# Feed-forward nets of a two-layer decoder: sums moved from GpSimd to VectorE, low parts by adding transfers

## The chip, the cores and the metric

The kernel runs on one core of a Trainium2 chip. The metric is the device time of one execution in microseconds, the median of several runs. TensorE (PE) multiplies, VectorE (DVE), ScalarE (ACT) and GpSimd (POOL) work element by element, SyncE (SP) issues the transfers.

## What is computed

```python
def _swiglu(h, w_gate_up, w_down):
    gu = h @ w_gate_up
    return (jax.nn.silu(gu[..., :D_FF]) * gu[..., D_FF:]) @ w_down
...
    for l in range(DEPTH):
        hn = _rmsnorm(h, attn_norm[l])
        ...
        h = h + _swiglu(_rmsnorm(h, ffn_norm[l]), ffn_w_gate_up[l], ffn_w_down[l])
    return _rmsnorm(h, final_norm)
```

The stream has 1024 tokens of 1024 values in float32, `D_FF` is 2816, and there are two layers: latent attention in layer 0, differential attention in layer 1, each followed by the feed-forward net shown.

## The kernel before

**Numbers in two parts.** TensorE multiplies in `float32r`, which keeps fewer digits than float32. So each operand is held as a high part (the value rounded) and a low part (the value less its high part), and a product takes three matmuls. `split` (L412) makes the two: ScalarE writes the high part, and VectorE, or GpSimd where `sub` says so, subtracts it from the source.

**Fewer products.** The nets use Strassen-Winograd: seven products of half-size blocks in place of eight, with sums of blocks of the weights and of the operands. `block_tail` (L1096) holds one layer's net. Its input is in seven operand lists `x[0]` to `x[6]`. A pair `p` of weight columns goes through `up(p)`: forms 0, 2, 3 and 4 as whole products (accumulators `pa`, `pc`), and form 1, 5 and 6 as `quarter_products`, which apply the scheme once more to 256-column pieces (accumulators `pb`). From pair `CUT` on (pair 4 in layer 0, pair 2 in layer 1) form 1 is in quarters too; before that it is whole. There are eleven pairs per layer. The first three pairs' forms are made ahead, during attention, by `prepare_columns` (L946), and are loaded from memory (`preh`, `prel`).

**Weight forms.** `Columns` makes the forms of a column: it loads blocks into `wr` tiles, `form` (L1237) makes a sum in place (`t` is form 3, then becomes form 2, then form 6), and `get` (L1256) splits it into `wh` and `wl`. With four blocks of rows (`np == 4`, the up weights) the sums ran on GpSimd, else on VectorE. The sums of `quarter_products` (tiles `qt`) ran on GpSimd.

**Down.** After the pairs, `down` and `down_last` multiply the activations by the down weights in four groups. `stage` loads a pair's activations from memory and makes their sums (tiles `stg`), and `place` (L1553) splits the seven of them; forms 2, 4 and 6 had their low parts on GpSimd. VectorE adds every product into the residual tiles `h`.

**Order.** Between `nc.start` and `nc.finish` the calls are only recorded. `Plan.finish` then sets the order on each engine from a table of costs (`Plan.cost`, L287 is the line at which all of them are issued, so L287 stands on almost every row). An engine runs its list in that order: an instruction that waits holds up all behind it on its engine.

Of the kernel before, what the change touches and what calls it, by code (L numbers as in the profile page):

```python
# [14 lines left out]
AF = mybir.ActivationFunctionType  # L15
# [177 lines left out]
class Plan:  # L193
# [100 lines left out]
    def cost(self, engine, name, n, dtype, psum, accum, size):  # L294

        if engine == "tensor":
            if name == "transpose":
                return 0.107, self.HOP
            return n * (1 if dtype == F32R else 6 if n <= 64 else 8) / 2400, self.HOP
        if engine == "scalar":  # L300
            return (0.05 if psum else 0.09) + n / 1200 + 0.19 * accum, self.HOP
        if engine == "vector":
            return 0.067 + n / 960 + 0.063 * (name == "scalar_tensor_tensor" and not psum), self.HOP
        if engine == "gpsimd":
            return (0.245 + n / 1200 if name == "tensor_scalar" else 0.15 + n / 475), self.HOP
        return max(0.45, size / 360e3), 2.2
# [64 lines left out]
def trunk(ctx: ExitStack, tc: tile.TileContext, A: dict):  # L371
# [34 lines left out]
    def f32(ap):  # L406
        return ap.bitcast(F32)
# [4 lines left out]
    def split(dst_hi, dst_lo, src, scale=1.0, sub=None):  # L412
        nc.scalar.activation(dst_hi, src, AF.Copy, scale=scale)
        if isinstance(scale, float) and scale == 1.0:
            (sub or nc.vector).tensor_tensor(dst_lo, src, f32(dst_hi), ALU.subtract)
        else:
            nc.vector.scalar_tensor_tensor(dst_lo, src, scale, f32(dst_hi), ALU.mult, ALU.subtract)

    def mm3(ps, parts):
        n = len(parts)  # L420
# [532 lines left out]
    def prepare_columns(layer, j, tags):  # L953


        kept = pre[layer, j] = {i: [dram.tile([P, HF], F32R, name="pre" + part) for part in "hl"] for i in early_forms(layer, j // 2)}
        t4 = kept["t4"] = dram.tile([P, HF], F32, name="pret")

        def load(i):
            t = tags.tile([P, HF], F32, "pb", "pb")  # L960
            nc.sync.dma_start(out=t, in_=A["wgu"][layer, j, :, i])
            return t

        def keep(i, src):
            pair = [tags.tile([P, HF], F32R, "p" + part, "p" + part) for part in "hl"]
            split(*pair, src, sub=nc.gpsimd)
            for d, t in zip(kept[i], pair):
                move(d, t)

        def sub(dst, a, b):  # L970
            nc.gpsimd.tensor_tensor(dst, a, b, ALU.subtract)

        t = tags.tile([P, HF], F32, "pt", "pt")
        nc.sync.dma_start(out=t, in_=A["wgu"][layer, j, :, 1])
        b0 = load(0)
        sub(t, t, b0)
        keep(0, b0)
        yield
        keep(3, t)
        b3 = load(3)  # L980
        sub(t, b3, t)
        yield
        keep(2, t)
        b2 = load(2)
        sub(t, b2, t)
        nc.sync.dma_start(out=t4, in_=t)
        yield
        if 1 in kept:
            keep(1, b2)
            yield  # L990
        b1, b3 = load(1), load(3)
        sub(b1, b3, b1)
        keep(4, b1)
        yield
# [135 lines left out]
    def block_tail(layer, half, resid, last, side_work=None, ahead=None, meanwhile=None):  # L1130
# [90 lines left out]
        class Columns:  # L1221
# [16 lines left out]
            def form(self, j):  # L1238
                if self.made is not None and j == 6:
                    return raw(self.made["t4"])  # L1240
                eng = nc.gpsimd if self.np == 4 else nc.vector
                b = self.block
                if j == 3:
                    self.t = raw()
                    return self.sub(self.t, b(1), b(0), eng)
                if j == 2:
                    return self.sub(self.t, b(3), self.t, eng)
                if j == 4:
                    return self.sub(b(1), b(3), b(1), eng)
                if j == 6:  # L1250
                    return self.sub(self.t, b(2), self.t, eng)
                return b({0: 0, 1: 2, 5: 3}[j])

            def get(self, i):
                if self.made is not None and self.forms[i] is None:
                    self.forms[i] = wtile()  # L1256
                    for t, d in zip(self.forms[i], self.made[i]):
                        move(t, d)
                while self.forms[i] is None:
                    j = next(self.order)  # L1260
                    src = self.form(j)
                    w = self.np * P
                    hi, lo = (t[:, :w] for t in (self.kept[j]() if j in self.kept else wtile()))
                    split(hi, lo, src[:, :w])
                    self.forms[j] = hi, lo
                return self.forms[i]

# [30 lines left out]
        def quarter_products(i, w0, w1, d0, d1):  # L1298

            t13, t24 = htile(7, 1, "qt"), htile(6, 1, "qt")  # L1300
            nc.gpsimd.tensor_tensor(t13[:, L], w1[:, L], w0[:, L], ALU.subtract)
            nc.gpsimd.tensor_tensor(t13[:, R], w1[:, R], w1[:, L], ALU.subtract)
            nc.gpsimd.tensor_tensor(t24[:, L], w1[:, R], t13[:, L], ALU.subtract)
            nc.gpsimd.tensor_tensor(t24[:, R], w0[:, R], t24[:, L], ALU.subtract)
            ws = []
            for s in (w0, t13, t24, w1):
                w = wtile()
                c = R if s is w1 else slice(0, HF)
                split(*(t[:, c] for t in w), s[:, c])
                ws.append(w)  # L1310
            part = lambda w, c: [t[:, c] for t in w]
            b11, b21, b22 = part(ws[0], L), part(ws[0], R), part(ws[3], R)
            t1, t3, t2, t4 = part(ws[1], L), part(ws[1], R), part(ws[2], L), part(ws[2], R)
            a11, a12, s4, a22, s1, s2, s3 = quarters[i]

            def mul(ps, xs, w, start):
                for k, (xh, xl) in enumerate(xs):
                    wh, wl = (t[:, k * P : (k + 1) * P] for t in w)
                    nc.tensor.matmul(ps, lhsT=wh, rhs=xh, start=start and k == 0, stop=False, skip_group_check=not start)
                    nc.tensor.matmul(ps, lhsT=wh, rhs=xl, start=False, stop=False, skip_group_check=not start)  # L1320
                    nc.tensor.matmul(ps, lhsT=wl, rhs=xh, start=False, stop=k == 1, skip_group_check=not start)

            def add(t, ps):
                nc.vector.tensor_tensor(t, t, ps, ALU.add)

            c11, c12, c21, c22 = d0[:, L], d1[:, L], d0[:, R], d1[:, R]
            a, b, c = (bank("pb")[:, L] for _ in range(3))
            mul(a, a11, b11, True)
            add(c11, a)
            mul(b, a12, b21, True)  # L1330
            add(c11, b)
            mul(c, s1, t1, True)
            add(c22, c)
            mul(a, s2, t2, False)
            add(c12, a)
            mul(c, s4, b22, False)
            add(c12, c)
            mul(a, s3, t3, False)
            add(c22, a)
            mul(a, a22, t4, False)  # L1340
            add(c21, a)
# [211 lines left out]

        def place(xs, p, i):
            t = dtile(i, SLOTS[p])
            split(*t, staged[p][i], sub=nc.vector if i in (0, 1, 3, 5) else nc.gpsimd)
            xs[i].append(t)


# [4 lines left out]
        for k in range(4):  # L1564
            a21, a22 = h[1][k], h[1][k + 4]
            for t, kk in ((a21, k), (a22, k + 4)):
                nc.vector.scalar_tensor_tensor(t, t, gain(f"ffn{layer}", kk), r, ALU.mult, ALU.mult)
            s1, s2 = (tags.tile([P, HF], F32, "st", "st") for _ in range(2))
            a11, a12 = h[0][k], h[0][k + 4]
            forms = [a11, a12, s2, s1, a21, a12, a22]  # L1570
            for _ in sums(a11, a12, a21, a22, s1, s2, a12, (nc.vector, nc.gpsimd)):
                pass
            for i in range(2, 5):
                x[i][k] = xtile(i, k)
                split(*x[i][k], forms[i], sub=nc.vector if i < 4 else nc.gpsimd)
        for _ in range(6):
            next(ups[0])
        for _ in range(4):
# [1 line left out]
        for i, src in ((5, h[0][4:]), (6, h[1][4:])):  # L1580
            for k in range(4):
                x[i][k] = xtile(i, k)
                c = L if k < 2 else slice(0, HF)
                split(*(t[:, c] for t in x[i][k]), src[k][:, c], sub=nc.vector if i == 5 else nc.gpsimd)
            quarter_operands(i, src.__getitem__, nc.vector if i == 5 else nc.gpsimd)

        def whole(k):

# [395 lines left out]
```

## Time and profile before

| | us |
|---|---|
| runs | 2487.7, 2488.48, 2494.13; median 2488.48 |
| the profiled execution, its own time | 2489.24 |
| its span in the trace | 2487.0 |
| TensorE busy | 2334.4 (94%) |
| VectorE busy | 1928.1 (78%) |
| ScalarE busy | 1167.5 (47%) |
| GpSimd busy | 1124.2 (45%) |

Busy times overlap, so they don't add up to the span. TensorE is busy for nearly all of it; the question of every stage is what TensorE waits for in the rest. The nets lie at 503 to 1180 us (layer 0) and 1790 to 2452 us (layer 1) of the span: in each the pairs come first and the down product last.

### The profile page before, as it was taken

The numbers are of one execution on the slowest core, as the hardware profiler recorded it, in microseconds if no ns is written. First come the engines' busy times: TensorE is split into PE (matmuls) and PEld (weight loads), VectorE is DVE, ScalarE is ACT, GpSimd is POOL, SyncE is SP. The second block draws the span as 40 slices with busy tenths as digits, with TensorE's granted clock in tenths as the row PEclk, the third lists the DMA queues.
The fourth block names the chain that finished last, engine by engine and source line by source line (L and its number), as shares of the span: only waits on it lengthen the run. The fifth ranks groups of instructions, "written<-read, shape, count | busy, mean of one in ns | idle before, by whom it ended". The sixth has DMA issues, their size and how long they took to land. (4 is left out here: it accounts for less than half of the span.)

```text
span 2487.0 us, 38148 instructions
## 1 busy us (share of the span) xinstructions
PE 2334.4 (94%) x12776; PEld 1998.5 (80%) x12776; DVE 1928.1 (78%) x3685; ACT 1167.5 (47%) x2323; POOL 1124.2 (45%) x979
## 2 busy tenths in 40 slices
PE   9989999989899997999999999999889999988997
PEld 7879898768788886777889898888678888876776
DVE  7855564597978789999686767676688787799997
ACT  5356554344444444343465555454344444454442
POOL 3256532262656552123377765443365565542212
PEclk9999999999999999999999999999999999999999
DMA  6166673746322235322376653463834222244321
GB/s 185 43 204 200 200 247 110 229 134 209 97 79 91 75 106 185 104 92 88 95 220 196 212 167 118 142 224 109 278 115 147 79 88 77 82 151 152 103 67 70
DMA packets 202003, 346.36 MB, mean 139 GB/s; under 512 B 24656, under 2 KB 57680, under 8 KB 201808
## 3 DMA queue, kind: packets, MB, share of 16 engines
q1 hardware_dynamic: 201808, 343.93, 44.0%
q8 instruction: 101, 1.65, 0.3%
q14 instruction: 94, 0.77, 0.1%
HBM read 239.89 MB, written 95.03 MB: 135 GB/s over the span
## 5 line engine op out<-in xcount | busy, mean ns | idle before, releaser
L287 ACT ACTIVATE wh<-wr 128x512 fp32r<-128x512 f32 (+2 forms) x530 | 287.3, 550 | 443.6 <-PE pb L287 130.8
L287 DVE TENSOR_TENSOR wl<-wr,wh 128x512 fp32r<-128x512 f32 (+2 forms) x530 | 393.1, 755 | 32.8 <-ACT wh L287 32.2
L287 PE MATMUL pa<-xh,wh 128*128 128x512 f32 (+1 forms) x850 | 339.0, 400 | 34.7 <-DVE h L287 14.7
L287 PE MATMUL pa<-xh,wl 128*128 128x512 f32 (+1 forms) x850 | 337.3, 398 | 17.7 <-DVE wl L287 16.4
L287 PE MATMUL pa<-xl,wh 128*128 128x512 f32 (+1 forms) x850 | 336.0, 396 | 4.3 <-DVE xl L287 4.3
L287 PE MATMUL pb<-xh,wh 128*128 128x256 f32 (+1 forms) x976 | 291.9, 302 | 23.0 <-DVE s L287 17.1
L287 PE MATMUL pb<-xl,wh 128*128 128x256 f32 (+1 forms) x976 | 291.1, 299 | 0.0
L287 PE MATMUL pb<-xh,wl 128*128 128x256 f32 (+1 forms) x976 | 290.0, 299 | 0.1
L287 POOL TENSOR_TENSOR wr<-wr 128x512 f32<-128x512 f32 x128 | 179.0, 1398 | 173.5 <-DMA wr<-wgu 85.2
L287 POOL TENSOR_TENSOR xl<-stg,xh 128x512 fp32r<-128x512 f32 x66 | 110.3, 1688 | 305.2 <-ACT xh L287 164.7
L287 PEld LDWEIGHTS pa<-xh,wh 128*128 128x128 f32 x850 | 162.9, 192 | 76.7 <-DVE h L287 15.1
L287 PEld LDWEIGHTS pb<-xh,wh 128*128 128x128 f32 x976 | 186.3, 192 | 45.7 <-DVE s L287 26.4
L287 PEld LDWEIGHTS pa<-xh,wl 128*128 128x128 f32 x850 | 162.4, 191 | 56.3 <-DVE wl L287 24.0
L287 PEld LDWEIGHTS pb<-xl,wh 128*128 128x128 f32 x976 | 187.1, 192 | 13.5
L287 PEld LDWEIGHTS pb<-xh,wl 128*128 128x128 f32 x976 | 186.3, 192 | 6.2 <-DVE wl L287 0.8
L287 PEld LDWEIGHTS pa<-xl,wh 128*128 128x128 f32 x850 | 163.0, 192 | 35.0 <-DVE xl L287 6.0
L287 POOL TENSOR_SCALAR p<-p,tot 128x640 f32<-128x640 f32 (+7 forms) x128 | 99.0, 774 | 182.5 <-DVE tot L287 119.2
L287 ACT ACTIVATE p<-sc,nmax 128x128 f32<-128x128 f32 (+7 forms) x192 | 141.9, 741 | 78.0 <-DVE nmax L287 46.1
L287 POOL TENSOR_TENSOR qt<-wr 128x256 f32<-128x256 f32 x120 | 102.9, 877 | 125.6 <-DVE wl L287 108.0
L287 PE MATMUL pc<-xh,wh 128*128 128x512 f32 x352 | 138.8, 397 | 9.0 <-DVE h L287 8.8
L287 DVE TENSOR_TENSOR s<-s,pb 128x256 f32<-128x256 f32 (+1 forms) x278 | 115.4, 425 | 38.5 <-PE pb L287 35.4
L287 PE MATMUL pc<-xl,wh 128*128 128x512 f32 x352 | 139.6, 397 | 3.0 <-DVE xl L287 3.0
(296 smaller groups left out, 6496.9 us busy)
## 6 DMA issues: line engine op xcount, KB each, us to landing
wr<-wgu SPq DMA_DIRECT2D x142, 256.0 KB, 3.2
act_d<-s SPq DMA_DIRECT2D x88, 256.0 KB, 2.7
stg<-act_d SPq DMA_DIRECT2D x88, 256.0 KB, 3.0
wr<-wd SPq DMA_DIRECT2D x96, 192.0 KB, 2.4
pb<-wgu SPq DMA_DIRECT2D x60, 256.0 KB, 3.9
preh<-ph SPq DMA_DIRECT2D x58, 256.0 KB, 3.1
prel<-pl SPq DMA_DIRECT2D x58, 256.0 KB, 2.7
wh<-preh SPq DMA_DIRECT2D x58, 256.0 KB, 4.8
```

What stands on the lines that cost most here:

```text
L287: return getattr(getattr(self.nc, engine), name)(*map(put, args), **{k: put(a) for k, a in kw.items()})
```

## The change

```diff
@@ Plan.cost
+        if name == "dma_start" and engine == "gpsimd":
+            return 0.9, 3.8
@@ new, beside split
+    def low_by_transfer(dst_hi, dst_lo, src):
+
+        nc.scalar.activation(dst_hi, src, AF.Copy)
+        nc.scalar.activation(dst_lo, src, AF.Copy, scale=-1.0)
+        nc.gpsimd.dma_start(out=f32(dst_lo), in_=src, accum_op=ALU.add)
@@ prepare_columns
-            nc.gpsimd.tensor_tensor(dst, a, b, ALU.subtract)
+            nc.vector.tensor_tensor(dst, a, b, ALU.subtract)
@@ Columns.form, Columns.get
-                eng = nc.gpsimd if self.np == 4 else nc.vector
+                eng = nc.vector
-                    split(hi, lo, src[:, :w])
+                    (low_by_transfer if self.np == 4 else split)(hi, lo, src[:, :w])
@@ quarter_products (four lines like this one)
-            nc.gpsimd.tensor_tensor(t13[:, L], w1[:, L], w0[:, L], ALU.subtract)
+            nc.vector.tensor_tensor(t13[:, L], w1[:, L], w0[:, L], ALU.subtract)
@@ place
-            split(*t, staged[p][i], sub=nc.vector if i in (0, 1, 3, 5) else nc.gpsimd)
+            if i in (2, 6):
+                low_by_transfer(*t, staged[p][i])
+            else:
+                split(*t, staged[p][i], sub=nc.vector)
@@ operands before the first pair
-            for _ in sums(a11, a12, a21, a22, s1, s2, a12, (nc.vector, nc.gpsimd)):
+            for _ in sums(a11, a12, a21, a22, s1, s2, a12, (nc.vector, nc.vector)):
-                split(*x[i][k], forms[i], sub=nc.vector if i < 4 else nc.gpsimd)
+                (split if i < 4 else low_by_transfer)(*x[i][k], forms[i])
-                split(*(t[:, c] for t in x[i][k]), src[k][:, c], sub=nc.vector if i == 5 else nc.gpsimd)
-            quarter_operands(i, src.__getitem__, nc.vector if i == 5 else nc.gpsimd)
+                split(*(t[:, c] for t in x[i][k]), src[k][:, c])
+            quarter_operands(i, src.__getitem__, nc.vector)
```

With `low_by_transfer` ScalarE writes the rounded value and then the rounded value negated, and a transfer issued from GpSimd adds the source to the second: the low part is the same as before.

In the whole program the instructions of TensorE are the same in number. GpSimd loses 530 tensor instructions and gains 182 transfers: 130 of whole weight forms (`wl<-wr`), 44 of staged activations (`xl<-stg`), 8 of operands (`xl<-h`). ScalarE gains 182 activations of 128x512. VectorE loses 130 low parts of 128x512 (`wl<-wr,wh`) and gains 218 sums or low parts of 128x512, 48 of them in attention, and 260 of 128x256, 240 of them the `qt` sums.

The plan makes a new order out of it. GpSimd, end of the list, the last pairs and the down product of layer 1; before:

```order
L287 TENSOR_TENSOR wr<-wr 128x512 x4
L287 TENSOR_TENSOR xl<-stg,xh 128x512
L287 TENSOR_TENSOR qt<-wr 128x256 x2
L287 TENSOR_TENSOR qt<-wr,qt 128x256
L287 TENSOR_TENSOR xl<-stg,xh 128x512
L287 TENSOR_TENSOR qt<-wr,qt 128x256
L287 TENSOR_TENSOR xl<-stg,xh 128x512 x31
L287 TENSOR_TENSOR ss<-ss,sq 128x512 x6
```

and in the change, from the operands of layer 1's net to the same place:

```order
L287 TENSOR_TENSOR xl<-h,xh 128x512 x8
L287 DMA xl<-h 128x512 x4
L287 TENSOR_TENSOR whole<-xh,xl 128x512 x4
L287 DMA wl<-wr 128x512 x64
L287 DMA xl<-stg 128x512 x22
L287 TENSOR_TENSOR ss<-ss,sq 128x512 x6
```

Between the operands and the last norm GpSimd now holds the four `whole` sums of form 1 and transfers, nothing else.

VectorE in the change, a stretch between two pairs of layer 1, with what each waits for (DMASW is a semaphore of a transfer issued from GpSimd; `s_22265` collects a pair's gate):

```order
L287 TENSOR_TENSOR wr<-wr 128x512 [waits DMASW2_49]
L287 TENSOR_TENSOR s_22265<-s_22265,pb 128x256 [waits PE_49]
L287 TENSOR_TENSOR s_22265<-s_22265,pb 128x256 [waits DVE_49,PE_49]
L287 TENSOR_TENSOR s_22265<-s_22265,pb 128x256 [waits PE_49]
L287 TENSOR_TENSOR wr<-wr 128x512 [waits DMASW4_49]
L287 TENSOR_TENSOR wl<-wr,wh 128x512 [waits Activation_49]
L287 TENSOR_TENSOR wl<-qt,wh 128x512 [waits Activation_49]
```

The sums in place now stand in VectorE's list among the additions that set TensorE's accumulators free, and they wait for the transfer that still reads the tile.

ScalarE in the change at the start of a pair (`pa_22152` is the accumulator of the pair before, `wl_22534` the low part of the new pair's form 0):

```order
L287 ACTIVATE s2_22484<-pa_22152 128x512
L287 ACTIVATE wh_22518<-wr_22311 128x512
L287 ACTIVATE sg_22527<-pa_22152 128x512
L287 ACTIVATE wl_22534<-wr_22311 128x512
L287 ACTIVATE wh_22542<-wr_22354 128x512
L287 ACTIVATE wl_22552<-wr_22354 128x512
```

Ahead of the second half of such a pair's low part stands the copy `sg` of the last whole product. In TensorE's list 48 quarter matmuls (128x256) and 4 whole ones (128x512) lie between the last matmul of that product and the first that reads `wl_22534`.

## Rows read from the trace of the kernel before

**Rows 1.** The page, its span and TensorE's busy time.

```profile
span 2487.0 us, 38148 instructions
...
PE 2334.4 (94%) x12776; PEld 1998.5 (80%) x12776; DVE 1928.1 (78%) x3685; ACT 1167.5 (47%) x2323; POOL 1124.2 (45%) x979
```

**Rows 2.** Stages: length, busy PE, PEld, DVE, ACT, POOL; clock, DMA share, GB/s.

```profile
503.00:594.00 91.00, 79.95 (x406) 66.27 (x405) 78.15 (x132) 40.13 (x79) 49.07 (x46) 0.96 0.49 158
594.00:679.00 85.00, 77.41 (x415) 66.50 (x414) 76.54 (x131) 36.11 (x68) 44.54 (x43) 0.98 0.39 119
679.00:905.00 226.00, 221.45 (x1301) 193.35 (x1300) 177.55 (x289) 107.32 (x187) 124.66 (x117) 1.00 0.28 84
905.00:960.00 55.00, 43.34 (x239) 36.90 (x238) 50.36 (x81) 29.50 (x58) 28.08 (x21) 0.94 0.52 170
960.00:1180.00 220.00, 203.48 (x858) 161.81 (x857) 210.09 (x353) 87.53 (x171) 54.77 (x37) 0.98 0.33 105
1250.00:1660.00 410.00, 392.29 (x2435) 349.50 (x2434) 300.01 (x753) 226.94 (x504) 246.17 (x216) 0.98 0.57 177
...
1790.00:1880.00 90.00, 78.07 (x406) 65.43 (x406) 78.40 (x121) 39.43 (x79) 53.63 (x50) 0.96 0.49 156
1880.00:2186.00 306.00, 300.68 (x1768) 262.63 (x1767) 244.37 (x400) 145.75 (x259) 167.10 (x157) 1.00 0.30 91
2186.00:2242.00 56.00, 45.05 (x242) 38.54 (x241) 50.47 (x82) 29.94 (x59) 28.78 (x21) 0.92 0.51 167
2242.00:2452.00 210.00, 196.14 (x832) 156.72 (x831) 200.64 (x343) 83.32 (x164) 46.63 (x30) 0.98 0.30 91
```

**Rows 3.** TensorE's waits over the span: us in total, times, longest.

```profile
PE pb L287 <- DVE s L287: 17.1, 7, 6.2
PE pa L287 <- DVE wl L287: 16.4, 17, 3.2
```

**Rows 4.** Timeline between two pairs of layer 1: start, duration, engine, what.

```profile
1960.06 0.32 SPq L287 DMA_DIRECT2D act_d<-s  x1
...
1960.72 1.28 POOL L287 TENSOR_TENSOR wr<-wr 128x512 f32<-128x512 f32 x1 [1.23 <-DVE wl L287]
1960.89 1.65 DVE L287 TENSOR_TENSOR wl<-wr,wh 128x512 fp32r<-128x512 f32 x1
...
1961.24 0.28 PE L287 MATMUL pb<-xl,wh 128*128 128x256 f32 x1
...
1961.36 0.28 PE L287 MATMUL pb<-xh,wl 128*128 128x256 f32 x1
...
1962.60 0.50 PE L287 MATMUL pa<-xh,wl 128*128 128x512 f32 x1 [0.60 <-DVE wl L287]
```

**Rows 5.** Groups by form, whole span: count, busy us, mean ns, idle before.

```profile
L287 DVE TENSOR_TENSOR wl<-wr,wh 128x512 fp32r<-128x512 f32 x258 | 232.2, 909 | 32.4 <-ACT wh L287 31.9 <-issue 0.2
...
L287 ACT ACTIVATE wh<-wr 128x512 fp32r<-128x512 f32 x258 | 162.3, 630 | 213.8 <-PE pb L287 95.7 <-DMA wr<-wo 33.4 <-POOL wr L287 32.0
...
L287 DVE TENSOR_TENSOR s<-s,pb 128x256 f32<-128x256 f32 x266 | 107.5, 413 | 36.9 <-PE pb L287 35.1
...
L287 DVE TENSOR_TENSOR wl<-qt,wh 128x512 fp32r<-128x512 f32 x120 | 102.6, 867 | 25.5 <-ACT wh L287 25.4
...
L287 DVE TENSOR_TENSOR h<-h,pa 128x512 f32<-128x512 f32 x136 | 90.5, 677 | 12.5 <-PE pa L287 12.2
...
L287 DVE TENSOR_TENSOR s<-s,sg 128x512 f32<-128x512 f32 x44 | 53.5, 1242 | 1.3 <-ACT sg L287 1.3
```

**Rows 6.** The same view, VectorE in the down product of layer 0 (960 to 1180 us).

```profile
L287 DVE TENSOR_TENSOR wl<-wr,wh 128x384 fp32r<-128x384 f32 x78 | 47.6, 623 | 0.1
...
L287 DVE TENSOR_TENSOR xl<-stg,xh 128x512 fp32r<-128x512 f32 x32 | 29.4, 932 | 0.0
```

**Rows 7.** Transfers: issue, count, KB each, median us from issue to landing.

```profile
wr<-pret SPq DMA_DIRECT2D x12, 256.0 KB, 5.5
...
out<-h SPq DMA_DIRECT2D x8, 256.0 KB, 2.0
```

More of the change, by code (lines that the diff above doesn't have):

```diff
@@ L1300, in quarter_products @@
             t13, t24 = htile(7, 1, "qt"), htile(6, 1, "qt")
-            nc.gpsimd.tensor_tensor(t13[:, L], w1[:, L], w0[:, L], ALU.subtract)
-            nc.gpsimd.tensor_tensor(t13[:, R], w1[:, R], w1[:, L], ALU.subtract)
-            nc.gpsimd.tensor_tensor(t24[:, L], w1[:, R], t13[:, L], ALU.subtract)
-            nc.gpsimd.tensor_tensor(t24[:, R], w0[:, R], t24[:, L], ALU.subtract)
+            nc.vector.tensor_tensor(t13[:, L], w1[:, L], w0[:, L], ALU.subtract)
+            nc.vector.tensor_tensor(t13[:, R], w1[:, R], w1[:, L], ALU.subtract)
+            nc.vector.tensor_tensor(t24[:, L], w1[:, R], t13[:, L], ALU.subtract)
+            nc.vector.tensor_tensor(t24[:, R], w0[:, R], t24[:, L], ALU.subtract)
             ws = []
```

## The prediction

> **What bounds the kernel now.** I read the page first, then busy times by stage, then TensorE's waits, a timeline at one of them, and the groups by form. TensorE is busy for 94% of 2487.0 us [rows 1], so no change of the other engines can give back more than its idle time and what a lowered clock costs. The stages say where that lies [rows 2]: length less TensorE's busy time is 11.1, 7.6, 4.6, 11.7 and 16.5 us in the five stages of layer 0's net, and 11.9, 5.3, 11.0 and 13.9 us in the four of layer 1's, 93.4 us together. A clock column below 1.00 means that part of the stage ran at 1.2 GHz instead of 2.4; a share of 0.96 over 91 us is a loss of 0.04 x 91 = 3.6 us. Over the same nine stages this is 3.6 + 1.7 + 0 + 3.3 + 4.4 + 3.6 + 0 + 4.5 + 4.2 = 25.3 us. So 119 us is the ceiling in the nets; the low clock stands in the stages with idle time and not in the two without long waits.
>
> What TensorE waits for there is VectorE: additions that empty accumulators, and low parts [rows 3]. In the down products it is busy 210.1 of 220 us and 200.6 of 210 us, 96%, which makes it the bound of those stages; between pairs in the middle of the nets it has 177.6 of 226 us and room [rows 2].
>
> And VectorE is slowed by GpSimd. At 1960.72 us GpSimd starts a subtraction; the low part that VectorE starts at 1960.89 takes 1.65 us, and TensorE waits 0.60 us for it [rows 4]. With one operand in PSUM the same size takes 677 ns on average; the three forms with both operands in SBUF take 909, 867 and 1242 ns [rows 5]. Excess over 677: 258 x 0.232 + 120 x 0.190 + 44 x 0.565 = 59.9 + 22.8 + 24.9 = 107.6 us. The Trainium skill has this as a rule (SBUF — State Buffer, section Who interferes with whom): a VectorE instruction with two SBUF inputs and a GpSimd instruction that reads SBUF exclude each other for a whole instruction. The trace agrees, with 1.65 us against 0.677.
>
> **The change part by part.** *VectorE's sum.* In the nets, besides what attention gets, 218 - 48 - 130 = 40 instructions of 128x512 more, at 0.677, and 260 of 128x256 at 0.413 [rows 5]: 27.1 + 107.4 = 134.5 us. Against it stand the 107.6 us of excess and that of smaller groups, two of which I read in one down product [rows 6]: 32 x (0.932 - 0.677) = 8.2 us, and 78 x (0.623 - 0.545) = 6.1 us, where 0.545 is halfway between 0.413 and 0.677. VectorE therefore gets no less work in the whole. What changes is where and when: the 240 `qt` sums lie in the pairs, where VectorE has room, and the excess leaves the down products and the turns, where it has none.
>
> *Down products.* Per layer nine `place` calls of form 4 come to VectorE there, 9 x 0.677 = 6.1 us; 14.3 us of excess go by the two rows named, more by the others. VectorE's net relief is 8 us of 220 by these two rows, more by groups not read. While it is 96% busy TensorE's waits on it shrink by about as much, and with them the low clock. Lost there are 16.5 + 4.4 and 13.9 + 4.2 us; I take 10 us per layer: **-20** (bounds 0 and -39).
>
> *Turns from pairs to down* (905 to 960, 2186 to 2242 us). Lost: 11.7 + 3.3 and 11.0 + 4.5 us, most of it in single waits of up to 6.2 us on `s` [rows 3] behind VectorE's list. Three low parts in seven leave GpSimd, one of them for VectorE. I take a third: **-10** (bounds 0 and -30).
>
> *First pairs* (503 to 679, 1790 to 1880 us). VectorE has 78 of 91 us and gets about 8 sums of 0.677 and 28 of 0.413, 17 us per layer; the excess that leaves here I did not count. Of 14.7 + 9.3 + 15.5 us lost I take **-5** (bounds +10 and -20).
>
> *Steady pairs.* Lost are 4.6 + 5.3 us [rows 2], in waits like the one of 0.60 us shown [rows 4]. Now the low part of form 0 comes through ScalarE and a transfer. TensorE has 48 quarter and 4 whole matmuls to do meanwhile; quarters follow each other by 0.12 us [rows 4], whole ones by twice that: 6.7 us. Of these ScalarE takes two activations, 2 x 0.63 = 1.3 us less a little overlap [rows 5], so about 5.5 us remain for issue and landing. The trace has no transfer from GpSimd and none that adds. Bounds for 256 KB: 2.0 us, the quickest, and 5.5 us, the slowest [rows 7]; for the issue 0.32 us, SP's, and 1.28 us, a whole GpSimd instruction [rows 4]. I take 4.0, twice the quick one because two tiles are read, and 0.9: 4.9 us, in time. So less than half of what is lost comes back: **-4** (bounds -10 and, at 5.5 + 1.28, +1.3 us in each of the 16 pairs whose forms are not made ahead = +21).
>
> The Trainium skill prices a GpSimd transfer alone at 2.0 us plus bytes over 436 GB/s (DMA: Bandwidth & Descriptors, section Anatomy of one DMA — SWDGE path), an estimate of 2.6 us here; by it the transfer would be in time as well, and no run yet shows it.
>
> *ScalarE.* 182 activations of 0.63 us are 115 us; it is idle for half of each stage (145.8 busy of 306) [rows 2], so they are hidden but come ahead of copies of accumulators: **+2** (bounds 0 and +15). *DMA.* Its share is 0.28 to 0.30 in the steady pairs [rows 2]; eight more transfers per pair hide in that, and loads of `wr` wait for them: **+3** (bounds 0 and +12).
>
> *Attention.* 48 sums go from GpSimd to VectorE, 33 us at 0.677, up to 79 us if each is stopped as in [rows 4], because softmax work stays on GpSimd. In layer 1 VectorE is busy 300 of 410 us [rows 2], so there is cover; without it they would cost their length. **+3** (bounds -5 and +15).
>
> Sum: -20 - 10 - 5 - 4 + 2 + 3 + 3 = -31 us on 2489.24 us, the profiled execution's own time (2.2 us over its span, 0.8 us over the median): **2458 us**.
>
> **The rivals.** *Late transfers (slower).* If issue and landing take 7.5 us, form 0 is late by 2.0 us in 16 pairs, and the next form, which has about 1 us more time, by about 1.0: 48 us. VectorE suffers too: its sums in place wait for the same transfers, and the additions to `s` that TensorE needs stand behind them. With the gain of 31 kept elsewhere at 27: 2489 + 48 - 27 = 2510 us. It decides from about 6.4 us on, where 0.9 x 16 plus a little on the second form and VectorE's waits eats the 27. For it: rows of 5.5 us exist; against: quiet DMA queues in these stages.
>
> *Only moved (no change).* VectorE's 134.5 us of new work is as much as the excess that leaves; if the new list meets the accumulators as badly, the waits merely stand elsewhere: 2485 to 2493 us. For it: the sum above; against: the down products, where the balance is clearly downward.
>
> *GpSimd still blocks.* If issuing a transfer stops VectorE as a subtraction did, 182 issues of 0.9 us are 164 us, and with half of that as excess VectorE's list grows by 82 + 134.5 - 107.6 = 109 us. In the steady pairs it has 48 and 62 us of room [rows 2], in the other stages almost none; if a quarter reaches TensorE, that is 27 us: 2516 us. For it: both are work of GpSimd; against: an issue is short (SP's 0.32 us) beside a subtraction's 1.28 [rows 4]. The Trainium skill has a trap of the reverse kind (SBUF — State Buffer, The "DVE blocks DMA" trap): VectorE in two-port modes starves GpSimd of writing descriptors, and `tensor_tensor` has no such mode; if it held here, the transfers would be late, the first rival.
>
> **How the numbers follow.** The forecast has 64 in 100, with its own range of 2415 to 2480; late transfers 16, only moved 13, GpSimd still blocks 5, and 2 for attention or the first pairs costing more than the rest gives (2500 us). Within 0.3% of 2488 us (7.5 us), about what a measurement of this kernel can tell from no change, lies "only moved": 0.13. Faster by more is the forecast, 0.64; slower are the other three, 0.23. The range takes in the ceiling's two thirds, 2489 - 79 = 2410, and the first rival's 2510.
>
> **What would show it.** In the changed profile the groups of two SBUF operands should fall to about 680 ns, VectorE's busy share in the down products to about 90%, its idle time there should show, and TensorE's idle time in down and turns should fall by about a third or half. TensorE's waits should not name `wl<-wr` transfers. The prediction is wrong if landings of the adding transfers come later than 5 us, if VectorE's waits name them, or if the 909 ns stay.

## The result, and the profile after

The change takes 2426.56 us, median of four runs (2422.76 to 2435.62), against 2491.11 us before in the runs beside them: a ratio of 0.975, 95% interval 0.9726 to 0.9774. It is faster by 2.5%, twice the forecast's size and inside its range. The profiled execution took 2435.62 us, the slowest of its four, so the two traces differ by 53 us and the medians by 64.6. The sizes below are those of the traces.

The page of the change, as [rows 1], and its DMA queues (packets, MB, share of 16 engines' span):

```profile
span 2433.7 us, 38359 instructions
...
PE 2316.3 (95%) x12776; PEld 1994.8 (82%) x12776; DVE 1876.3 (77%) x4033; ACT 1246.4 (51%) x2505; POOL 663.6 (27%) x631
...
q1 hardware_dynamic: 201808, 343.93, 44.4%
q0 software_dynamic: 26208, 47.72, 11.5%
```

To compare stages I cut both traces at the same points of the work, the issues of the same `act_d<-s` transfers. Before, cut in this way (columns as in [rows 2]): six steady pairs of layer 0, its turn to the down product and that product, then eight pairs of layer 1, its turn and its down product.

```profile
679.00:911.00 232.00, 226.97 (x1335) 197.98 (x1333) 183.55 (x297) 111.67 (x195) 129.02 (x120) 1.00 0.28 86
911.00:961.00 50.00, 38.83 (x207) 33.02 (x208) 45.36 (x74) 25.15 (x50) 24.73 (x17) 0.92 0.52 170
961.00:1179.00 218.00, 201.48 (x850) 160.15 (x849) 208.71 (x349) 86.90 (x170) 53.53 (x36) 0.98 0.34 106
1883.00:2192.00 309.00, 303.62 (x1786) 264.93 (x1784) 247.37 (x401) 147.52 (x261) 171.12 (x159) 1.00 0.29 91
2192.00:2242.00 50.00, 39.11 (x204) 33.54 (x205) 44.47 (x74) 25.54 (x51) 24.02 (x17) 0.91 0.52 171
2242.00:2456.00 214.00, 200.14 (x866) 160.72 (x865) 202.88 (x348) 85.20 (x168) 47.87 (x32) 0.98 0.30 90
```

The change, the same six stages:

```profile
669.00:893.00 224.00, 222.96 (x1335) 198.47 (x1335) 171.00 (x369) 128.88 (x241) 41.27 (x48) 1.00 0.61 142
893.00:937.00 44.00, 39.37 (x217) 33.09 (x215) 37.14 (x77) 30.99 (x62) 8.58 (x10) 0.96 0.87 237
937.00:1150.00 213.00, 202.71 (x854) 162.09 (x854) 200.17 (x366) 94.82 (x188) 30.55 (x28) 0.97 0.48 136
1859.00:2153.00 294.00, 293.38 (x1757) 261.53 (x1756) 225.53 (x488) 170.25 (x317) 52.26 (x60) 1.00 0.60 142
2153.00:2194.00 41.00, 38.18 (x217) 32.02 (x215) 37.14 (x78) 30.66 (x62) 8.71 (x10) 1.00 0.90 246
2194.00:2403.00 209.00, 198.45 (x871) 160.55 (x872) 194.65 (x364) 92.94 (x186) 23.23 (x24) 0.98 0.44 122
```

The pairs in the middle are shorter by 8 and 15 us, the turns by 6 and 9, the down products by 5 each. Read layer 0's pairs: 1335 matmuls are recorded in both, and TensorE's *busy* time fell with its idle time, by 4.0 and 4.0 us. VectorE gives layer 0's down product 200 us of 213, 94%; whether it is still the bound there is what e9 tests.

TensorE's waits in the change (as [rows 3]):

```profile
PE pb L287 <- DVE wl L287: 12.7, 2, 6.3
...
PE pa L287 <- DVE h L287: 11.5, 6, 4.2
...
PE pa L287 <- DVE wl L287: 4.6, 8, 1.3
...
PE pa L287 <- DMA wl<-wr: 2.9, 3, 1.9
...
PE pb L287 <- DVE s L287: 2.0, 3, 1.0
```

The 17.1 us on `s` are 2.0 now, the 16.4 on `wl` 4.6. The first two rows hold new waits: two of 6.3 us, one in the first pairs of each layer, and one of 4.2 us, below. VectorE's groups by form (as [rows 5]), over the span:

```profile
L287 DVE TENSOR_TENSOR wl<-wr,wh 128x512 fp32r<-128x512 f32 x128 | 98.1, 773 | 60.0 <-ACT wh L287 58.4 <-PE psp L287 0.5 <-issue 0.4
L287 DVE TENSOR_TENSOR wr<-wr 128x512 f32<-128x512 f32 x128 | 87.8, 687 | 20.1 <-DMA wl<-wr 11.9 <-DMA wr<-wgu 8.1
L287 DVE TENSOR_TENSOR wl<-qt,wh 128x512 fp32r<-128x512 f32 x120 | 82.7, 691 | 0.4 <-ACT wh L287 0.4
```

and in layer 0's down product, 937 to 1150 us (as [rows 6]):

```profile
L287 DVE TENSOR_TENSOR wl<-wr,wh 128x384 fp32r<-128x384 f32 x78 | 44.5, 586 | 0.0
L287 DVE TENSOR_TENSOR h<-h,pa 128x512 f32<-128x512 f32 x66 | 44.2, 681 | 11.5 <-PE pa L287 7.8 <-DMA h<-h_mid 3.4
L287 DVE TENSOR_TENSOR xl<-stg,xh 128x512 fp32r<-128x512 f32 x45 | 30.5, 702 | 0.0
```

The 867 and 932 ns are 691 and 702; the 773 ns over the span mix in attention, where GpSimd still works. The adding transfers (as [rows 7]):

```profile
wl<-wr POOLq DMA_DIRECT2D x130, 256.0 KB, 4.5
...
xl<-stg POOLq DMA_DIRECT2D x44, 256.0 KB, 4.5
```

The timeline at three places of layer 1 (as [rows 4]): an issue on GpSimd, four matmuls of a pair, the start of the down product.

```profile
1967.80 0.76 DVE L287 TENSOR_TENSOR qt<-wr 128x256 f32<-128x256 f32 x2
...
1968.23 0.89 POOL L287 DMA_DIRECT2D wl<-wr  x1 [0.66 <-PE pa L287]
1968.47 0.42 DVE L287 TENSOR_TENSOR qt<-wr,qt 128x256 f32<-128x256 f32 x1
...
1978.48 0.39 PE L287 MATMUL pa<-xh,wl 128*128 128x512 f32 x1
1978.71 0.39 PE L287 MATMUL pa<-xh,wh 128*128 128x512 f32 x1
1978.94 0.39 PE L287 MATMUL pa<-xl,wh 128*128 128x512 f32 x1
1979.16 0.39 PE L287 MATMUL pa<-xh,wl 128*128 128x512 f32 x1
...
2196.86 0.69 DVE L287 TENSOR_TENSOR h<-h,pa 128x512 f32<-128x512 f32 x1 [4.45 <-DMA h<-h_mid]
...
2197.60 0.80 PE L287 MATMUL pa<-xh,wh 128*128 128x512 f32 x1 [4.17 <-DVE h L287]
```

The issue lies beside two sums, and neither is longer for it. The matmuls are 0.39 us long in the trace and follow each other by 0.23: one that starts up to 0.16 us late leaves no idle time at all. Adding up by how much each start comes after the regular distance (0.227 us behind a 128x512 matmul, 0.114 to 0.117 behind a 128x256) shows the size of it: in the steady pairs before, TensorE started 9.1 and 10.8 us late in all, of which only 4.5 and 5.2 us show as idle; in the change it is 1.8 and 1.3 us.

### The profile page after: what moved, and what is told of

Same layout as the page of the kernel before. It is cut to its first block, busy times and chain, and to the rows that moved or that the text cites. A ratio compares the mean times of both kernels' runs of the same rounds, so it can differ in the third digit from the quotient of the medians.

```text
span 2433.7 us, 38359 instructions
## 1 busy us (share of the span) xinstructions
PE 2316.3 (95%) x12776; PEld 1994.8 (82%) x12776; DVE 1876.3 (77%) x4033; ACT 1246.4 (51%) x2505; POOL 663.6 (27%) x631
## 3 DMA queue, kind: packets, MB, share of 16 engines
q1 hardware_dynamic: 201808, 343.93, 44.4%
q0 software_dynamic: 26208, 47.72, 11.5%
## 4 chain that ended last, share of the span: by engine, by line
PE 73%; DVE 13%; DMA 8%; issue 2%; ACT 2%; POOL 1%; SPq 1%; DVEq 0%; POOLq 0%; ACTq 0%
PE pa L287 22%; PE pb L287 14%; PE pc L287 8%; PE psp L287 7%; PE sc L287 5%; PE psv L287 4%; PE pswo L287 4%; PE pso L287 4%; DVE h L287 2%; PE tp L287 2%; DVE wl L287 2%; PE acc L287 1%; DVE xl L287 1%; PE psr L287 1%; PE ps L287 1%
## 5 line engine op out<-in xcount | busy, mean ns | idle before, releaser
L287 PE MATMUL pa<-xh,wh 128*128 128x512 f32 (+1 forms) x850 | 333.7, 397 | 18.3 <-DVE h L287 11.3
L287 PE MATMUL pa<-xh,wl 128*128 128x512 f32 (+1 forms) x850 | 330.7, 395 | 8.3 <-DVE wl L287 4.6
L287 DVE TENSOR_TENSOR wl<-wr,wh 128x384 fp32r<-128x384 f32 (+2 forms) x400 | 233.8, 596 | 81.9 <-ACT wh L287 80.3
L287 POOL DMA_DIRECT2D wl<-wr x130 | 112.6, 889 | 483.1 <-ACT wl L287 270.2
L287 PEld LDWEIGHTS pb<-xh,wl 128*128 128x128 f32 x976 | 185.6, 191 | 19.6 <-DVE wl L287 13.5
L287 DVE TENSOR_TENSOR wr<-wr 128x512 f32<-128x512 f32 (+2 forms) x256 | 154.1, 607 | 20.2 <-DMA wl<-wr 11.9
L287 PE MATMUL pc<-xh,wl 128*128 128x512 f32 x352 | 139.0, 395 | 3.0 <-DVE wl L287 2.7
```

The costliest lines, as they stand in the source:

```text
L287: return getattr(getattr(self.nc, engine), name)(*map(put, args), **{k: put(a) for k, a in kw.items()})
```

## The experiments

Two theories. *Reads*: the gain is that GpSimd no longer reads SBUF beside VectorE's sums. *Transfers*: it is that whole low parts have left VectorE. The table has all kernels; stage lengths are read at the same cuts as above, in us, layer 0 plus layer 1 (first pairs: four and three; steady pairs: six and seven; the attention between the nets), and can be off by 1 us. All but the before row have the ratio to the runs of before on the same chip.

| kernel | median, us | ratio, 95% interval | first pairs | steady pairs | turns | downs | attention |
|---|---|---|---|---|---|---|---|
| before | 2488 to 2491 | | 184+136 | 232+271 | 50+50 | 218+214 | 606 |
| the change | 2426.56 | 0.975, 0.9726 to 0.9774 | 172+137 | 224+258 | 44+41 | 213+209 | 608 |
| e1_sums_only | 2448.1 | 0.9841, 0.9825 to 0.9857 | 171+136 | 223+257 | 41+41 | 221+216 | 613 |
| e2_transfers_only | 2540.14 | 1.0211, 1.0194 to 1.0227 | 187+134 | 260+314 | 47+47 | 210+206 | 610 |
| e3_reads_beside | 2499.94 | 1.0052, 1.0033 to 1.007 | 216+165 | 221+257 | 42+42 | 213+208 | 604 |
| e4_writes_beside | 2429.13 | 0.9761, 0.9746 to 0.9775 | 169+135 | 222+257 | 43+42 | 212+209 | 607 |
| e5_attention_back | 2438.58 | 0.98, 0.978 to 0.982 | 172+137 | 223+258 | 43+43 | 210+207 | 619 |
| e6_down_weights_too | 2483.15 | 0.9978, 0.9961 to 0.9994 | 173+135 | 223+258 | 42+40 | 237+233 | 604 |
| e7_first_operands_back | 2428.76 | 0.9762, 0.9741 to 0.9784 | 175+136 | 221+258 | 43+42 | 211+210 | 607 |
| e8_staged_back | 2457.07 | 0.9877, 0.9856 to 0.9898 | 172+138 | 222+258 | 48+47 | 221+217 | 606 |
| e9_staged_all_by_transfer | 2434.89 | 0.9788, 0.9773 to 0.9803 | 171+136 | 224+258 | 42+41 | 213+212 | 607 |
| e10_plan_counts_later | 2452.16 | 0.9851, 0.9834 to 0.9867 | 173+133 | 235+268 | 50+48 | 208+206 | 606 |
| e11_plan_counts_earlier | 2433.19 | 0.977, 0.9753 to 0.9787 | 175+135 | 225+261 | 42+43 | 212+207 | 605 |
| e12_quarter_sums_back | 2448.76 | 0.9843, 0.9825 to 0.9861 | 177+136 | 221+268 | 48+47 | 211+208 | 606 |

**The two halves apart.** e1: every adding transfer is a `split` on VectorE again.

```diff
-                    (low_by_transfer if self.np == 4 else split)(hi, lo, src[:, :w])
+                    split(hi, lo, src[:, :w])
```

> All the change's sums on VectorE, but every low part by a VectorE subtraction, no transfer. It leaves GpSimd as free of reading SBUF in the nets as the change does, and VectorE gets 182 more subtractions of 0.68 us, 124 us. Theory A (the gain is that VectorE is no longer stopped by GpSimd): groups with two SBUF operands at about 0.69 us as in the change, and most of the gain in the steady pairs where VectorE had 23% of its time free; with 8 x 0.68 = 5.4 us more work in a pair of 37 us VectorE stays just under its limit: 2435 to 2465 us. Theory B (the gain is the work that the transfers take from VectorE): no gain or a loss, 2490 us or more.

It keeps 40 of the 62 us that the ratio of the change stands for. VectorE's groups are as quick as in the change, though its list is longer:

```profile
L287 DVE TENSOR_TENSOR xl<-stg,xh 128x512 fp32r<-128x512 f32 x154 | 102.4, 688 | 0.0
L287 DVE TENSOR_TENSOR h<-h,pa 128x512 f32<-128x512 f32 x136 | 90.3, 677 | 8.4 <-PE pa L287 7.9
```

Pairs and turns are as short as in the change; the downs are 437 us, longer than before (432). So taking the sums and low parts off GpSimd makes the gain in pairs and turns by itself, and the transfers make that in the downs. The attention is 5 us longer than in the change, and why is open. e2: the sums are on GpSimd again, the transfers stay.

```diff
-                eng = nc.vector
+                eng = nc.gpsimd if self.np == 4 else nc.vector
```

> All low parts that the change gives to transfers, but the sums stay on GpSimd as before. VectorE loses 130 subtractions, 88 us. Theory A: groups with two SBUF operands stay slow (over 0.8 us) and the time is 2465 to 2490 us. Theory B: most of the gain is here, 2425 to 2445 us.

Slower than before, which no theory said. The groups stay slow as A had it (`wl<-qt` 883 ns); the downs are short, the steady pairs 71 us longer than before. GpSimd's groups by form show what is new:

```profile
L287 POOL TENSOR_TENSOR wr<-wr 128x512 f32<-128x512 f32 x128 | 173.7, 1358 | 204.0 <-DMA wl<-wr 183.4 <-issue 7.8 <-DMA wr<-wgu 6.5
```

A sum in place waits on GpSimd for the transfer that still reads its tile, 183.4 us in all, and the next issues stand behind it. The delay can be followed to TensorE: in layer 1's steady pairs GpSimd waits 82.6 us for `wl<-wr`, ScalarE 46.5 us for GpSimd's `wr`, and TensorE 19.1 us for ScalarE's `wh`.

**Reads and writes of GpSimd.** e3 adds two sums on a 128x256 scratch tile, which nothing reads, behind every adding transfer in the code; e4 three fills of the tile.

```diff
         nc.gpsimd.dma_start(out=f32(dst_lo), in_=src, accum_op=ALU.add)
+        for _ in range(2):
+            nc.gpsimd.tensor_tensor(idle[0], idle[0], idle[0], ALU.add)
```

> The change, with two additions of a 128x256 scratch tile on GpSimd (0.74 us each before) after each of the 182 transfers; they read and write SBUF and feed nothing. Theory A: the two-operand groups of VectorE rise from 0.69 us to 0.78 or more, TensorE waits for low parts and sums again, and 182 x 1.5 us of GpSimd work take back a third or more of the gain: 2445 to 2475 us. Theory B: GpSimd has over 70% idle in the nets, the time stays within 0.4% of 2427 us.

> The same, with three fills of the scratch tile on GpSimd in place of the two additions: GpSimd is as busy or nearly so, writes SBUF and reads nothing. If what stops VectorE is GpSimd's reading, two-operand groups stay at 0.69 us and the time at 2427 us within 0.4%. If any work on GpSimd stops it (or delays the issue of the transfers), it loses as much as the run with additions.

The scratch work has no input but itself, so the plan set much of it early: 168 of e3's 364 sums, and 153 of e4's 546 fills, in layer 0's first pairs. So they do not lie beside each transfer, and the test is what happens where they do lie. e3, its groups from 500 to 715 us:

```profile
L287 POOL TENSOR_TENSOR idle<-idle 128x256 f32<-128x256 f32 x168 | 131.0, 780 | 11.6
...
L287 DVE TENSOR_TENSOR wl<-qt,wh 128x512 fp32r<-128x512 f32 x18 | 16.3, 913 | 0.3 <-ACT wh L287 0.2
L287 DVE TENSOR_TENSOR xl<-h,xh 128x256 fp32r<-128x256 f32 x20 | 15.5, 811 | 0.0
```

The change, from 500 to 669 us:

```profile
L287 DVE TENSOR_TENSOR xl<-h,xh 128x256 fp32r<-128x256 f32 x20 | 7.5, 417 | 0.4 <-ACT xh L287 0.4
```

e4, in the same stretch:

```profile
L287 POOL MEMSET idle<- 128x256 f32 x153 | 54.5, 356 | 7.4
...
L287 DVE TENSOR_TENSOR wl<-qt,wh 128x512 fp32r<-128x512 f32 x18 | 12.1, 683 | 2.8 <-ACT wh L287 2.8
L287 DVE TENSOR_TENSOR xl<-h,xh 128x256 fp32r<-128x256 f32 x20 | 7.5, 416 | 0.0
```

Beside reads the 128x256 low part takes 811 ns, beside fills 416, and 417 in the change. All of e3's loss lies in the first pairs, 44 and 28 us longer than in the change; no other stage is longer by more than 1 us. It is VectorE that TensorE waits for there, 29.7 us in layer 0's, and transfers `wl<-wr` only 3.1 us, so a late issue is not what costs. With fills nothing is lost. The fills kept GpSimd busy for 54.5 of 169 us and the sums for 131.0 of 215, so they are about half as dense, but nothing of the slowing is left. The Trainium skill (SBUF — State Buffer, section Who interferes with whom) says this: a VectorE instruction with two SBUF inputs contends with a GpSimd instruction that reads SBUF, not with one that only writes it. Both runs agree, with 811 and 416 ns. Only 10 of e3's sums lie in the steady pairs and none in the turns and downs, so it speaks for the first pairs alone.

**Parts undone one by one.** e5: the sums of the forms made ahead, in attention.

```diff
 prepare_columns
-            nc.vector.tensor_tensor(dst, a, b, ALU.subtract)
+            nc.gpsimd.tensor_tensor(dst, a, b, ALU.subtract)
```

> The change, with the 48 sums of the weight forms made ahead, which lie in attention, back on GpSimd; all else as in the change. A, the prediction's term: these sums cost VectorE 33 us of length that attention covers, and their move was worth between -5 and +5 us: 2421 to 2432 us, the groups of the nets unchanged at about 690 ns. B, rival: attention is where GpSimd's reads hurt as well, since VectorE has two-operand work there too; then the time rises by 10 us or more, 2437 or above, and the mean of VectorE's two-operand groups in attention rises above 800 ns.

12 us slower, by the time theory B; the attention between the nets takes 619 us in place of 608. But B's cause is not shown: `wl<-wr` there has 869 ns in both kernels, and TensorE's waits name one of 7.0 us at the start of layer 1's attention that neither the change nor before has:

```profile
PE sc L287 <- DVE ks L369: 7.0, 1, 7.0
```

Before, with these sums on GpSimd, attention took 606 us. What the part is worth depends on the order around it; its cause stays open. e7: the first operands (half of the sums, low parts of forms 4 to 6, quarter operands of form 6).

```diff
-            quarter_operands(i, src.__getitem__, nc.vector)
+            quarter_operands(i, src.__getitem__, nc.vector if i == 5 else nc.gpsimd)
```

> The change, with the operands ahead of the first pair (half of the sums, the low parts of forms 4 to 6, the quarter operands of form 6) back on GpSimd. A: the two waits of 6.3 us for a first quarter's low part come from VectorE's longer list there and go away; the first pairs of layer 1 get their 4 us back: 2415 to 2424 us. B, rival: GpSimd's reads come back beside VectorE's work in the first pairs and cost as much as the list did: 2425 to 2445 us, with VectorE's groups between the net's start and the third pair again at 900 ns or more.

The same time as the change, in the range of B. The two waits of 6.3 us go, as A said, and two on `s` come (9.2 us in all, 4.7 the longest). GpSimd's reads do slow VectorE again, as B said: the eight low parts `xl<-st` of layer 0 take 1430 ns in place of 685. So the part is worth nothing either way. e8: the staged low parts.

```diff
-            if i in (2, 6):
-                low_by_transfer(*t, staged[p][i])
-            else:
-                split(*t, staged[p][i], sub=nc.vector)
+            split(*t, staged[p][i], sub=nc.vector if i in (0, 1, 3, 5) else nc.gpsimd)
```

> The change, with the low parts of staged activations 2, 4 and 6 back on GpSimd as before. A: the down products' and turns' gain, some 25 us for the two layers, comes from these low parts leaving GpSimd: 2440 to 2455 us, low parts in the down products at 900 ns and more, the down products at about 218 and 214 us. B, rival: VectorE's list is the bound of the down products in either case, so what stopping costs it is given back by the shorter list: 2420 to 2432 us; then the gain of the down products has another source.

A, and a little more than its range: 31 us slower by the medians; in the trace turns are 9 and downs 17 us longer.

```profile
L287 DVE TENSOR_TENSOR xl<-stg,xh 128x512 fp32r<-128x512 f32 x88 | 74.8, 860 | 0.0
```

VectorE is busy for 212.4 us of layer 0's down product with 357 instructions, where the change has 200.2 with 366. e12: the `qt` sums.

```diff
-            nc.vector.tensor_tensor(t13[:, L], w1[:, L], w0[:, L], ALU.subtract)
+            nc.gpsimd.tensor_tensor(t13[:, L], w1[:, L], w0[:, L], ALU.subtract)
```

> The change, with the 240 sums qt of the quarter products back on GpSimd; the sums of the weight forms stay on VectorE. A: GpSimd's reads in the pairs stop VectorE again, and the short waits between pairs, which hide under the matmuls' modelled lengths, come back: a steady pair of layer 1 takes 38 us or more in place of 36.75, 2440 to 2455 us. B, rival: the pairs have room on VectorE either way (171 of 224 us busy), the sums on GpSimd cost nothing: 2422 to 2432 us.

A by the time, 22 us slower. Layer 1's steady pairs take 268 us, 38.4 a pair, and the turns are 10 us longer; `wr<-wr`, on VectorE in both, is slowed from 687 ns:

```profile
L287 DVE TENSOR_TENSOR wr<-wr 128x512 f32<-128x512 f32 x128 | 107.3, 839 | 20.7 <-DMA wr<-wgu 9.7 <-DMA wl<-wr 9.0 <-DVE s L287 1.7
```

But layer 0's steady pairs are no longer for it (221 us, 224 in the change), though `wr<-wr` takes 811 ns there too: a slowed VectorE costs time only where TensorE has to wait for it, and that hangs on the order as well.

**More of the same.** e6 makes the low parts of the down weights by transfer as well, e9 those of staged form 4.

```diff
-                    (low_by_transfer if self.np == 4 else split)(hi, lo, src[:, :w])
+                    low_by_transfer(hi, lo, src[:, :w])
```

> The change, and the low parts of the down weights (128x384, some 78 in each down product) are made by ScalarE and an adding transfer as well. A: VectorE is the bound of the down products (200 of 213 us busy); 78 x 0.574 = 45 us leave it in each, so its share falls to about 75%, and of the 21 us that TensorE does not work there and the few us of low clock half or more come back: 2400 to 2416 us. B, rival: the down products are bound by the chain of a weight column (load, high part, low part, product), and the transfer makes it longer by 3 to 4 us: TensorE then waits for wl<-wr transfers, 2430 to 2480 us. Between the two the wait shown decides.

> The change, with staged form 4 by an adding transfer as well (22 instructions of VectorE fewer, 11 in each down product, 690 ns each). A: VectorE, 94% busy in the down products, is still their bound after the change, so 15 us less on it give back 5 to 12 us: 2414 to 2422 us. B, rival: what is left there is the wait for the first operands and for DMA (the DMA share rises from 0.48 to some 0.56): 2423 to 2435 us.

e6 loses almost the whole gain by the medians; the profiled execution was the fastest of its ten (2471.89 us), and what it loses lies in the downs. Its window of layer 0's down product, and TensorE's waits:

```profile
935.00:1170.00 235.00, 211.45 (x871) 166.10 (x870) 158.10 (x255) 135.11 (x294) 122.71 (x137) 0.96 0.97 208
```

```profile
PE pa L287 <- DMA wl<-wr: 27.9, 21, 3.2
PE pc L287 <- DMA wl<-wr: 19.5, 8, 6.2
```

VectorE falls to 158 of 235 us as A said, and the DMA share rises from 0.48 to 0.97: the DMA engines are the bound now. The waits are those that B named, with full DMA engines behind them and not only the longer chain that B gave; the median is 3 us past B's range. e9 is 0.4% slower than the change by the ratios, whose intervals just touch: B. VectorE is busy for 194.5 us of layer 0's down product, 6 us less than in the change, and the product is no shorter, so VectorE's list is not the only bound there. More of its waits are for `stg<-act_d` loads (13.5 us in its groups, 3.0 in the change).

**Order alone.** e10 and e11 change one number of the table of costs.

```diff
         if name == "dma_start" and engine == "gpsimd":
-            return 0.9, 3.8
+            return 0.9, 6.0
```

> The change, with the table of costs counting an adding transfer's arrival 6.0 us after its issue ends in place of 3.8; the work is the same, the order is not. A: the landings of 4.5 us from issue that the trace shows agree with 0.9 + 3.8, so another figure can only make the order worse or leave it: 2425 to 2445 us. B, rival: transfers are the last thing that TensorE waits for between pairs, and an order that gives them more time is faster: 2405 to 2422 us.

> The change, with the table of costs counting an adding transfer's arrival 3.0 us after its issue ends in place of 3.8; the work is the same, the order is not. A: the order of the change fits the landings of 4.5 us from issue that the trace shows, and a lower figure puts readers ahead of their transfers: TensorE or VectorE waits for wl<-wr transfers, 2432 to 2450 us. B, rival: as the counting at 6.0 cost 25 us by an order that loads the weights later, a lower figure goes on to gain: 2405 to 2421 us.

With 6.0 the same instructions, as quick as in the change (`wl<-qt` 690 ns), take 25 us more: the steady pairs are as long as before, 503 us, and the turns 98; the downs are shorter by 7. Neither range holds it. TensorE waits 15 times for ScalarE's copies `s`, where the change has one such wait of 0.2 us:

```profile
PE pa L287 <- ACT s L287: 9.4, 15, 0.7
```

With 3.0 nothing is gained: the time is at the lower edge of A's, and the interval overlaps the change's. The waits that A named do come, on VectorE: its sums in place wait 32.4 us for `wl<-wr`, 11.9 us in the change.

No kernel here beats the change.

## Why the prediction was right, and where its sizes were not

The mechanism held: groups of two SBUF operands fell to about 690 ns, and with GpSimd's reads put back they rise again (e3, e8, e12). VectorE's balance was mis-sized: "no less work in the whole" rests on 107.6 us of excess, but its busy time fell by 51.8 us although 88 more instructions of 128x512 and 260 of 128x256 came to it, 167 us at the prediction's own 0.677 and 0.413. So some 219 us of stopping went, about twice what was counted. The signs that it named came only in part: turns and down products lost 46% of TensorE's idle time (52.4 to 28.3 us), but VectorE's waits do name the adding transfers (11.9 us), and TensorE's do too (2.9 us); both are small. The terms of the sum, as the traces have them:

- **Steady pairs, forecast -4, measured -21.** This step failed. It took the idle time shown, 4.6 + 5.3 us, for all that could be lost there; the ceiling of 119 us rests on the same reading. But a matmul's length in the trace (0.39 us) is longer than the distance to the next (0.23), so short waits stand in TensorE's busy time: in layer 0's pairs it fell by 4.0 us with 1335 matmuls in both. By the distances from start to start 19.9 us were lost, and 3.1 are left; a few of the 21 us are matmuls that the new order puts on the other side of a cut (1555 recorded in layer 1's seven pairs before, 1539 in the change). The -10 that the step gave as its bound was wrong for the same reason. The late transfers that it set against the gain did not come: 4.5 us from the start of the issue to landing, against 4.9 assumed, and 2.9 us of waits for `wl<-wr` in the whole span.
- **Down products, forecast -20, measured -11.** This step failed too. VectorE's relief came in the size named, 208.7 to 200.2 us in layer 0, 8 us. The step then gave TensorE 10, more than the relief, and VectorE's share, expected at 90%, is 94%. The low clock, 8.6 us of what the step counted as lost, did not come back: the granted clock is 0.97 and 0.98 in the two products, 0.98 in both before. Part is lost at the start: VectorE waits 3.4 and 4.5 us for `h<-h_mid` loads in the two layers, TensorE behind it 3.1 and 4.2, and [rows 5] have no such wait. There the DMA share in the turn is 0.87 and 0.90, against 0.52 and 0.51 in [rows 2]. In e1, with turns as short and no transfers, these waits are not there. So it is the DMA term's mechanism, a load kept waiting by the adding transfers, on other loads than it named and at two and a half times its +3. The relief itself needs the transfers: with every low part on VectorE the downs are 5 us longer than before (e1).
- **Turns, forecast -10, measured -15.** The mechanism is right; e8 and e12 bring back 9 and 10 us of it.
- **First pairs, forecast -5, measured -11**: -12 in layer 0, +1 in layer 1. This counts three pairs of layer 1; cut after two, as the prediction did, it is +3, and the steady pairs have -24. A new wait of 6.3 us stands in both layers. Undoing the part alone (e7) changes nothing, so the operands' move alone does not make the gain; with the `qt` sums back the first pairs are 4 us longer (e12), and the rest is not assigned.
- **Attention, forecast +3, measured +2.** The size agrees, but e5 shows that undoing it costs 12: what the part is worth is not settled, and the agreement may be luck.
- **ScalarE, +2**, has no row of its own; its waits do not appear among TensorE's larger ones in the change.

The five measured terms with the start of the net 2 us later make -53 before rounding. The forecast's -31 was 58% of it, and half of the 64.6 us of the medians. What it lacked is mostly the steady pairs; the down products, forecast at twice what came, hid some of that by luck.

The rivals: *late transfers* did not happen in the change but did in e6, through the DMA engines' share rather than through one transfer's time. *Only moved* is what e1 shows for the downs alone; its ground, as much new work as excess that leaves, fell with the 219 us. *GpSimd still blocks* is refuted by the issue of 0.89 us beside undisturbed sums, and by groups of 690 ns beside 182 issues. The Trainium skill's figure for a GpSimd transfer (DMA: Bandwidth & Descriptors, section Anatomy of one DMA — SWDGE path), an estimate of 2.6 us, is too short for these adding ones, which land 4.5 us after issue in the median.

## What to carry to other kernels

Where VectorE's instructions with two SBUF operands are longer than those with one operand in PSUM, look at what GpSimd reads beside them: moving its sums to VectorE can be worth more than they cost there, where TensorE waits for VectorE (layer 0 of e12 shows the other case). An adding transfer takes a low part off both engines, but only as long as the DMA engines have room and no sum in place that waits for its tile stands ahead of the next issue on the same engine (e2). TensorE's idle time in a profile is not the whole loss between its matmuls: compare stage lengths for equal matmul counts.

## What the runs showed of the hardware that was not expected

An adding transfer is dear for the DMA engines. 182 of them with 256 KB took 11.5% of 2433.7 us, 1.54 us of all sixteen engines each; at the rate of the other queue (343.93 MB in 44.4%) 256 KB take 0.82 us. With 156 more of 192 KB (and 56 of 128 KB and 12 more of 192 KB) the DMA share was 0.97 in the down product at 208 GB/s, while 237 GB/s were moved at 0.87 in the change's turn. And the order alone is worth 25 us (e10), as much as most single parts (31 in e8, 22 in e12, 12 in e5), so a part undone singly prices the part and the new order together.
